# Three mixtures of experts: weighted rows added to the residual in DRAM by indirect DMA, and each tile routed behind its own logits

## The chip, the cores and the metric

The kernel runs on one core of one Trainium2 chip, all in fp32. The metric is the device time of one execution in microseconds (us). The engines are named as the profile names them: PE is TensorE, DVE VectorE, ACT ScalarE, POOL GpSimd; SP is the engine that issues most of the transfers. The core's transfers share 16 DMA engines. SP and ACT issue into hardware queues, POOL into a software queue (q0), which the indirect transfers use.

## The reference

Two transformer blocks on 512 tokens (x, 512x1024) and, in the second block, 256 context tokens. Three times a mixture of 32 experts with top-2 routing stands behind a mixer. Cut to what matters:

```
x = x + hierarchical_moe(rms_norm(x, norm_ffn), ...)          # ma: 512 tokens, no gate
...
f = hier_moe(concat([h2, hc2]), *moe_args)                    # mb: 512 + 256 tokens
x   = x   + g2  * f[:512]
ctx = ctx + cg2 * f[512:]
...
f = hier_moe(h2, *moe_args)                                   # mc: 512 tokens
x = x + g2 * f
return rmsnorm(x, final_g)

def hier_moe(xt, wg, bg, we, be, w1, w3, w2):
    g_idx = argmax(xt @ wg + bg);  g_w = softmax(xt @ wg + bg)[g_idx]     # 4 groups
    top_p, top_e = top_k(softmax((xt @ we + be)[group g_idx]), 2)         # 8 experts each
    weights = g_w * top_p / sum(top_p)
    for each of the two experts e of a token:
        y[token] += weight * ((silu(x @ w1[e]) * (x @ w3[e])) @ w2[e])
```

The gate row g2 (cg2 for the context) has 1024 numbers and is the same for all tokens of its kind.

## The kernel before

The tokens lie in tiles of 128 on the partitions: NT = 4 tiles in ma and mc, 6 in mb (four of x, two of the context). A mixture has a head, a route, a loop over experts and an end.

**Head** (`moe_head`, L269). For each tile, as soon as the mixer before has finished it: norm (`nrm`), transposes (L260), logits on PE (L302), the bias added on DVE into `lg` (L303), and the normed rows stored in DRAM as H (L304); with `keep` the residual rows go to XD in DRAM (L306). The tile scheduler weaves these steps into the mixer's own work.

**Route** (`route`, L498). Once all tiles' logits are in `lg`, one batch of DVE operations on 128 x NT x 32 numbers picks groups and experts, counts with PE matmuls (L570, L574) how many tokens of lower number chose the same expert, and builds with one-hot matrices (L590, L592, matmul L594) tables by expert: `gtab`, which tokens to gather, `tabs`, their weights, `sidx`, where a result row goes, and `cnt`, how many tokens an expert has. The first gather needs `gtab` (cast L625).

**Loop** (`moe`). Per expert 6 MB of weights, six tiles of 1 MB, come by SP's queue into rings of tiles in SBUF (`open_ring`, `pump`): a ring's tile is loaded again when the expert that used it is done. Ahead of the loop the rings fill: 17 tiles in ma, 19 in mb and mc (later some of these tiles are withdrawn for other uses). `gather` fetches the token rows of the expert after next from H by an indirect DMA on POOL (L342), after a clear of the buffer (L348). `block` computes up to 64 tokens: gate and up matmuls (L386), silu (L391, L392), transposes, down matmuls (L404), scaling by the weight on ACT (`yf`, L406), and a scatter of the rows into Y in DRAM by an indirect DMA on POOL (L407). Y has a row for each token and choice, so that no two scatters write the same row. An expert with over 64 tokens runs a second block of 64 or 32 tokens, one with over 128 the loop `later`. In a block of 32 the result is held as 128 partitions x 256.

**End.** Behind expert 29 the loop of mb and mc also reads the residual rows XD into `xr` (L472) and the gate rows `g` into SBUF. After the last scatter each tile reads its two Y rows (L481); DVE adds them (L483) and multiplies by the gate (L484), POOL adds the result to `xr` (L485). In ma the residual has stayed in SBUF and DVE adds both (L487, L488). Then `after` works on each tile: norms for the next stage, or, after mc, the final rmsnorm and the store of the output (L1901, L1902).

The order inside `moe` is that of the code, by a manual schedule; the order outside it, heads and ends among them, is the scheduler's.

Of the kernel before, what the change touches and what calls it, by code (L numbers as in the profile page):

```python
# [6 lines left out]
F32 = mybir.dt.float32  # L7
F32R = mybir.dt.float32r
BF16 = mybir.dt.bfloat16
# [13 lines left out]
class K:  # L23
# [245 lines left out]
    def moe_head(self, tag, NT, wr, br, rows, keep=True, bufs=1):  # L269
# [5 lines left out]
        lg = sp.tile([128, NT, 36], F32, name=tag + "lg")  # L275
# [8 lines left out]
        self.head = tag, NT, st, s2, sp, lg, H  # L284
# [3 lines left out]
        def tile_(t, x, wait=1):  # L288
# [22 lines left out]
    def moe(self, ring, back=None, gate=None, after=None):  # L311
# [5 lines left out]
        tag, NT, st, s2, sp, lg, H = self.head  # L317
        T = NT * 128
        s2.close()
        with st:  # L320
            wk = st.enter_context(tc.tile_pool(reuse_waits="tile", name=tag + "w", bufs=2))
            Y = self.dr.tile([2 * T, D], F32, name=tag + "Y")
            self.ordered = True
            half = lambda n: self.ttile(n, F32)
            self.open_ring(ring, st, 192)
            back_ = (NT + 3) // 4 if gate else 0
            two = lambda n: (self.xtile(n), self.xtile(n))
            self.tleft.clear()
            self.open_ring(6 - (back_ + 1) // 2, self.tpair, 192)
            self.open_ring((back_ + 1) // 2, self.tpair, 192 - 24)  # L330
            if gate:
                self.open_ring(NT // 2, two, 192 - 24)
            if NT == 4:
                self.open_ring(1, two, 192 - 18)

            with ExitStack() as s3:
                rt = s3.enter_context(tc.tile_pool(reuse_waits="tile", name=tag + "r", bufs=1))
                pos, cnt, wid, tabs, sidx, gtab = self.route(tag, rt, sp, lg, NT)
            w2 = st.enter_context(tc.tile_pool(reuse_waits="tile", name=tag + "w2", bufs=1))

# [16 lines left out]
            def block(wk, n, src, xT, wt, si, fill=(), mid=()):  # L357
# [12 lines left out]
                sl = wk.tile([64, 512], F32, name=tag + "sl", tag="sl", bufs=1)  # L370
                sl = [sl[:, 256 * f:256 * f + 256] for f in range(f2)]
                aT = [None] * f2

                def turned(f):
                    pt = self.psumt([128, 128])
                    for k in range(2):
                        nc.tensor.transpose(pt[:, 64 * k:64 * k + 64], sl[f][:, k * 128:(k + 1) * 128], self.ident[0:64, 0:64])
# [32 lines left out]
            def at(i, e):  # L410
                return tabs[:, i, e:e + 1], sidx[:, i, e:e + 1]
# [1545 lines left out]
```

## Time and profile before

| | |
|---|---|
| median of 3 runs | 3354.36 us (3350.82 to 3358.08) |
| profiled execution, own time | 3355.64 us |
| its span in the trace | 3353.8 us |
| mean granted TensorE clock, share of full speed | 0.919 |
| busy: PE, DVE, ACT, POOL | 84%, 33%, 26%, 19% |
| DMA, mean over the span | 250 GB/s |

The profiled execution is 1.84 us longer by its own time than its span in the trace, and 1.3 us above the median of the runs. Busy shares are averages over stages that have different limits: mix1 (to about 670), ma (to 1227), the middle with mix2 (to about 1698), mb (to 2258), mix3 (to about 2722), mc (to 3317) and its end. What a stage waits for is read from windows of it.

### The profile page before, as it was taken

The page shows a single profiled execution, that of the slowest core. Times are in us where ns is not written, and L with a number is a line of the kernel's source. Part 1 is how long each engine was busy: PE and PEld are TensorE (multiplying, and loading weights), DVE is VectorE, ACT ScalarE, POOL GpSimd, SP SyncE. Part 2 cuts the span into 40 slices and gives each one's busy share as a digit, 9 for nine tenths or more (in the row PEclk, how much of TensorE's full clock was granted, in tenths as well). Part 3 has the DMA queues.
Part 4 walks back from the last instruction along what each step waited for, and adds up shares of the span by engine and source line. Part 5 has one row for each costly group of instructions (what it writes and reads, how often), then busy time and mean ns, then how long its engine had stood idle before and what let it go on. Part 6 is the DMA issues. An engine that isn't in the chain of part 4 may idle for free. (4 is left out here: it accounts for less than half of the span.)

```text
span 3353.8 us, 52397 instructions
## 1 busy us (share of the span) xinstructions
PE 2824.7 (84%) x20723; PEld 1945.2 (58%) x20723; DVE 1099.5 (33%) x2328; ACT 860.2 (26%) x1790; POOL 634.1 (19%) x701
## 2 busy tenths in 40 slices
PE   6998898878988879879868998875999867899884
PEld 5766777654544439857744555444877654555442
DVE  3666654331100026555431110116355441010003
ACT  3354211211111126334311111113244311111111
POOL 2111202111211103101012121114122121122111
PEclk7999999969999989969979999996999878999997
DMA  5243358489999973132079999984222273999996
GB/s 185 77 159 121 98 189 273 162 329 411 411 397 398 403 297 117 33 109 70 26 288 406 404 410 384 401 343 141 86 79 60 68 314 152 362 410 391 400 399 241
DMA packets 281904, 838.98 MB, mean 250 GB/s; under 512 B 60002, under 2 KB 118109, under 8 KB 238496
## 3 DMA queue, kind: packets, MB, share of 16 engines
q1 hardware_dynamic: 215872, 752.94, 58.4%
q0 software_dynamic: 32752, 60.57, 4.9%
q10 hardware_dynamic: 32752, 18.80, 2.1%
q8 instruction: 286, 4.69, 0.6%
q14 instruction: 242, 1.98, 0.2%
HBM read 823.93 MB, written 56.59 MB: 263 GB/s over the span
## 5 line engine op out<-in xcount | busy, mean ns | idle before, releaser
L386 PE MATMUL mm<-w,maxT 128*64 128x256 f32 x2048 | 266.4, 396 | 63.7 <-DMA w<-in_w_up_dram 34.6
L386 PE MATMUL mm<-w,mcxT 128*64 128x256 f32 x2048 | 262.8, 399 | 56.0 <-DMA w<-in_moe_w_dram 23.7
L386 PE MATMUL mm<-w,mbxT 128*64 128x256 f32 x2048 | 248.7, 397 | 41.1 <-PEq L455 34.2
L386 PEld LDWEIGHTS mm<-w,maxT 128*64 128x64 f32 x2048 | 157.9, 142 | 174.4 <-DMA w<-in_w_up_dram 51.6
L386 PEld LDWEIGHTS mm<-w,mcxT 128*64 128x64 f32 x2048 | 157.7, 143 | 162.6 <-issue 55.6
L386 PEld LDWEIGHTS mm<-w,mbxT 128*64 128x64 f32 x2048 | 157.4, 142 | 133.1 <-issue 60.5
L246 PE MATMUL mm<-lo,hT 128*128 128x256 f32 x560 | 160.3, 287 | 4.5 <-DVE lo L737 4.4
L244 PE MATMUL mm<-hi,hT 128*128 128x256 f32 x560 | 160.8, 288 | 2.9 <-DVE d_q L149 1.9
L245 PE MATMUL mm<-hi,hT 128*128 128x256 f32 x560 | 160.5, 287 | 0.6 <-DVE hT L202 0.6
L392 DVE TENSOR_TENSOR masl<-masl,mm 64x256 f32<-64x256 f32 x64 | 27.1, 423 | 320.4 <-ACT masl L391 320.4
L392 DVE TENSOR_TENSOR mcsl<-mcsl,mm 64x256 f32<-64x256 f32 x64 | 27.1, 423 | 309.8 <-ACT mcsl L391 309.8
L392 DVE TENSOR_TENSOR mbsl<-mbsl,mm 64x256 f32<-64x256 f32 x64 | 27.0, 423 | 283.9 <-ACT mbsl L391 283.9
L404 PE MATMUL mm<-w,mcaT 128*64 128x512 f32 x512 | 117.1, 599 | 2.7 <-DMA w<-in_moe_w_dram 2.7
L404 PE MATMUL mm<-w,mbaT 128*64 128x512 f32 x512 | 117.1, 599 | 1.7 <-DMA w<-in_moe_w_dram 1.7
L404 PE MATMUL mm<-w,maaT 128*64 128x512 f32 x512 | 117.1, 599 | 0.3 <-DMA w<-in_w_down_dram 0.3
L407 POOL DMA_INDIRECT mbY<-mbyf,mbsidx x38 | 38.0, 1000 | 399.8 <-ACTq L455 148.2
L407 POOL DMA_INDIRECT mcY<-mcyf,mcsidx x35 | 35.1, 1003 | 408.8 <-POOLq L455 163.1
L246 PEld LDWEIGHTS mm<-lo,hT 128*128 128x128 f32 x560 | 107.8, 193 | 5.7 <-DVE lo L737 5.7
L244 PEld LDWEIGHTS mm<-hi,hT 128*128 128x128 f32 x560 | 108.0, 193 | 3.8 <-DVE d_q L149 2.1
L245 PEld LDWEIGHTS mm<-hi,hT 128*128 128x128 f32 x560 | 108.0, 193 | 1.1 <-DVE hT L202 1.0
L245 PE MATMUL mm<-hT,lo 128*128 128x512 f32 x240 | 98.2, 409 | 6.7 <-DVE lo L737 6.6
L407 POOL DMA_INDIRECT maY<-mayf,masidx x32 | 32.7, 1022 | 373.4 <-ACTq L455 195.5
(710 smaller groups left out, 5915.1 us busy)
## 6 DMA issues: line engine op xcount, KB each, us to landing
w<-in_moe_w_dram SPq DMA_DIRECT2D x342, 1024.0 KB
w<-in_w_up_dram SPq DMA_DIRECT2D x64, 1024.0 KB
w<-in_w_down_dram SPq DMA_DIRECT2D x64, 1024.0 KB
w<-in_w_gate_dram SPq DMA_DIRECT2D x57, 1024.0 KB
w<-in_moe_w_dram SPq DMA_DIRECT2D x84, 512.0 KB
w<-in_ada_w_dram SPq DMA_DIRECT2D x34, 1024.0 KB
w<-in_w_in_dram SPq DMA_DIRECT2D x21, 1024.0 KB
w<-in_ada_w_dram SPq DMA_DIRECT2D x28, 512.0 KB
```

What stands on the lines that cost most here:

```text
L244: nc.tensor.matmul(out, l[0], r[0], start=first, stop=False)
L245: nc.tensor.matmul(out, l[1], r[0], start=False, stop=False)
L246: nc.tensor.matmul(out, l[0], r[1], start=False, stop=last)
L386: nc.tensor.matmul(gu[f][n * j:n * j + n], x_[:, k, :], w(j // (q // 2), k)[:, c:c + 256], start=(k == 0), stop=(k == 7))
L392: nc.vector.tensor_tensor(sl[f], sl[f], gu[f][64:128], op=OP.mult)
L404: nc.tensor.matmul(y[n * j:n * j + n], l, w(2, k)[:, c * j:c * j + c], start=(k == 0), stop=(k == 3))
L407: nc.gpsimd.indirect_dma_start(out=Y.rearrange("t (j f) -> (t j) f", f=c), out_offset=bass.IndirectOffsetOnAxis(ap=si, axis=0), in_=yf, in ...
```

## The change

Three things are changed together.

1. **Scatter.** Instead of writing to Y the scatter adds to XD, the residual rows in DRAM (`compute_op=OP.add`), each row as two halves of 512 numbers. So the residual rows are stored in ma too, the weights and the gate row are multiplied in before the scatter (in mc one DVE operation, in mb three, in ma the scaling on ACT as before), with the gate tiles `G` (128x512) loaded by ACT's queue ahead of the loop. Each scatter waits for the one before it, as it did on Y. At the end each tile only reads `xr` from XD, after the last scatter; the reads behind expert 29 are gone.
2. **Route.** `route` becomes a generator for one tile, run right behind the tile's logits in the head. It adds the tile's one-hot products into `acc`; `tables`, ahead of the loop, only turns `acc` into the tables. The two matmuls that count (`pc`) add to the counts of the tiles already routed.
3. **Tiles.** A block of 32 tokens holds its result as 128 partitions x 512 with a clear of `yf` on POOL before; the silu buffer is 128x256; the rings ahead of the loop hold 19 tiles in all three mixtures.

```diff
-            nc.vector.tensor_tensor(lg[:, t, :], pl, bt, op=OP.add)
             nc.gpsimd.dma_start(H[t * 128:(t + 1) * 128, :], h)
-            if keep:
-                self.store(t, x)
-            yield
+            self.store(t, x)
+            yield from self.route(t, pl, bt, rt)
...
-            self.open_ring(6 - (back_ + 1) // 2, self.tpair, 192)
-            self.open_ring((back_ + 1) // 2, self.tpair, 192 - 24)
-            if gate:
-                self.open_ring(NT // 2, two, 192 - 24)
-            if NT == 4:
-                self.open_ring(1, two, 192 - 18)
+            early = 0 if after is None else 1
+            self.open_ring(6 - early, self.tpair, 192)
+            self.open_ring(early, self.tpair, 192 - 24)
+            self.open_ring(2, two, 192)
+            self.open_ring(1, two, 192 - 18)
...
+            for v, row in enumerate(gate or ()):
+                G.append(w2.tile([128, 512], F32, name=f"{tag}G{v}"))
+                for j in range(2):
+                    nc.scalar.dma_start(G[v][64 * j:64 * j + 64], row[512 * j:512 * j + 512].partition_broadcast(64))
...
-                c = 1024 // q
-                y = self.psum([128, c])
+                y = self.psum([128, 512])
...
-                    for j in range(q):
-                        nc.tensor.matmul(y[n * j:n * j + n], l, w(2, k)[:, c * j:c * j + c], start=(k == 0), stop=(k == 3))
-                yf = wk.tile([128, c], F32, name=tag + f"yf{q}", tag="yf")
-                nc.scalar.activation(yf, y, AF.Copy, scale=wt)
-                nc.gpsimd.indirect_dma_start(out=Y.rearrange("t (j f) -> (t j) f", f=c), out_offset=bass.IndirectOffsetOnAxis(ap=si, axis=0),
-                                             in_=yf, in_offset=None, bounds_check=2 * T * q - 1, oob_is_err=False)
+                    for j in range(2):
+                        nc.tensor.matmul(y[64 * j:64 * j + n], l, w(2, k)[:, 512 * j:512 * j + 512], start=(k == 0), stop=(k == 3))
+                yf = wk.tile([128, 512], F32, name=tag + "yf", tag="yf")
+                if n < 64:
+                    nc.gpsimd.memset(yf, 0.0)
+                for r_ in [slice(0, 128)] if n == 64 else [slice(64 * j, 64 * j + n) for j in range(2)]:
+                    if not G:
+                        nc.scalar.activation(yf[r_], y[r_], AF.Copy, scale=wt[0][r_])
+                        continue
+                    nc.vector.scalar_tensor_tensor(yf[r_], y[r_], wt[0][r_], G[0][r_], OP.mult, OP.mult)
+                    if W == 2:
+                        nc.vector.scalar_tensor_tensor(y[r_], y[r_], wt[1][r_], G[1][r_], OP.mult, OP.mult)
+                        nc.vector.tensor_tensor(yf[r_], yf[r_], y[r_], op=OP.add)
+                nc.gpsimd.indirect_dma_start(out=self.XD[0:T].rearrange("t (j f) -> (t j) f", f=512), out_offset=bass.IndirectOffsetOnAxis(ap=si, axis=0),
+                                             in_=yf, in_offset=None, bounds_check=2 * T - 1, oob_is_err=False, compute_op=OP.add)
...
-                if e == 29 and gate:
-                    g = [gate(i, half(f"g{i}")) for i in range(1 + (NT > 4))]
-                    xs = [self.xtile("xr") for _ in range(NT)]
-                    for t in range(NT):
-                        nc.sync.dma_start(xs[t], self.XD[t * 128:(t + 1) * 128, :])
...
             for t in range(NT):
-                a, b = half("y0"), half("y1")
-                for k, o in enumerate((a, b)):
-                    nc.sync.dma_start(o, Y[k * T + t * 128:k * T + t * 128 + 128, :])
-                if gate:
-                    nc.vector.tensor_tensor(a, a, b, op=OP.add)
-                    nc.vector.tensor_tensor(a, a, g[t // 4], op=OP.mult)
-                    nc.gpsimd.tensor_tensor(xs[t], xs[t], a, op=OP.add)
-                else:
-                    nc.vector.tensor_tensor(a, a, b, op=OP.add)
-                    nc.vector.tensor_tensor(xs[t], xs[t], a, op=OP.add)
+                xs.append(self.xtile("xr"))
+                nc.sync.dma_start(xs[t], self.XD[t * 128:(t + 1) * 128, :])
                 ends.append(after(t, xs[t]))
```

The new route, cut to its steps (39 DVE operations a tile; `yield` marks where the scheduler may turn to other work):

```python
    def route(self, t, pl, bt, rt):
...
        nc.vector.tensor_tensor(lg, pl, bt, op=OP.add)
        nc.vector.tensor_reduce(mx, gl, AX.X, OP.max)
        nc.vector.tensor_scalar(ex, gl, mx, None, OP.subtract)
        nc.scalar.activation(ex, ex, AF.Exp, accum_out=gs)
...
        yield
        for k in range(2):
            nc.vector.tensor_reduce(v[:, k:k + 1], m, AX.X, OP.max)
            nc.vector.scalar_tensor_tensor(oh[k], m, v[:, k:k + 1], rev, OP.is_equal, OP.mult)
            nc.vector.tensor_reduce(q[:, k:k + 1], oh[k], AX.X, OP.max)
            nc.vector.tensor_scalar(oh[k], rev, q[:, k:k + 1], None, OP.is_equal)
...
        nc.vector.tensor_tensor(av[:, 2 * i], oh[0], oh[1], op=OP.add)
        pc = self.psum([128, 32])
        nc.tensor.matmul(pc, self.striu, av[:, 2 * i], start=True, stop=(i == 0))
        if i:
            nc.tensor.matmul(pc, self.ones, av[:, 2 * i - 1], start=False, stop=True)
...
        yield
        pw = self.psum([128, 32 * (1 + W)])
        for k in range(2):
            nc.vector.tensor_tensor(big, oh[k], pc, op=OP.mult)
            nc.vector.tensor_reduce(rk[:, k:k + 1], big, AX.X, OP.add)
            nc.vector.tensor_scalar(ohr, self.iota, rk[:, k:k + 1], None, OP.is_equal)
...
            nc.tensor.matmul(pw, ohr, rhs.rearrange("p a b -> p (a b)"), start=(k == 0), stop=(k == 1))
...
            nc.vector.tensor_tensor(accf, accf, pw, op=OP.add)
```

Where instructions stand is shown at three places. The first is PE ahead of mc, where the output projection of mix3 (L244 to L246) for the last tile meets the head's transposes (L260) and logits (L302). Before, the order is:

```order
L302 MATMUL mm<-mcwr,mchT 128x36 [waits DVE_49]
L302 MATMUL mm<-mcwr,mchT 128x36 x3
L244 MATMUL mm<-hi,o_oT_34246 128x512
L245 MATMUL mm<-hi,o_oT_34246 128x512
L246 MATMUL mm<-lo,o_oT_34246 128x512
```

In the change, after the same logits:

```order
L260 MATMUL tr<-c_ident,nh 128x128 [waits DVE_49]
L260 MATMUL tr<-c_ident,nh 128x128 x7
L549 LDWEIGHTS cc_striu
L549 MATMUL mm<-mcav,cc_striu 128x32 [waits DVE_49]
L260 MATMUL tr<-c_ident,nh 128x128 [waits DVE_49,PE_49]
L260 MATMUL tr<-c_ident,nh 128x128 x3
L260 MATMUL tr<-c_ident,nh 128x128 [waits PE_49]
L260 MATMUL tr<-c_ident,nh 128x128
L574 MATMUL mm<-mchT 128x64 [waits DVE_49] x2
L244 MATMUL mm<-hi,o_oT_34287 128x512
L245 MATMUL mm<-hi,o_oT_34287 128x512
L246 MATMUL mm<-lo,o_oT_34287 128x512
```

The routing matmuls of an earlier tile (L549 is `pc`, L574 `pw`), each of which waits for DVE, now stand ahead of output matmuls; before, all routing matmuls stood behind the last logits.

The second place is DVE ahead of ma. Before, between the logits' bias additions (L303) and the table there is one batched route, which begins behind the last tile's addition:

```order
L149 COPY mahT<-tr 128x512 [waits PE_49]
L303 TENSOR_TENSOR malg<-mm,mabr 128x36 [waits PE_49]
L505 TENSOR_REDUCE magm<-malg 128x4 [waits DVE_49]
L509 TENSOR_TENSOR mage<-malg,magm 128x16 [waits DVE_49]
L517 TENSOR_TENSOR mac_6109<-malg,magm 128x16
```

In the change (L519 is the bias addition, the scratch carries the name of the transposes' buffer, mahT) the end of a tile's route, the next tile's logits and a later tile's norm (nrs, nh) follow one another:

```order
L581 TENSOR_TENSOR mapos<-mahT 128x2
L572 TENSOR_TENSOR mahT<-mahT,mawid 128x64 [waits DVE_49] x2
L166 TENSOR_SCALAR nrs<-nss 128x1 [waits Activation_49]
L579 COPY maacc<-mm 128x64 [waits PE_49]
L519 TENSOR_TENSOR mahT<-mm,mabr 128x36 [waits PE_49]
L149 COPY mahT<-tr 128x512 [waits PE_49]
L522 TENSOR_REDUCE mahT<-mahT 128x1 [waits DVE_49]
L169 RECIPROCAL nrs<-nrs 128x1 [waits Activation_49]
L523 TENSOR_SCALAR mahT<-mahT 128x4 [waits DVE_49]
L526 SCALAR_TENSOR_TENSOR mahT<-mahT,c_rev_5882 128x4
L182 SCALAR_TENSOR_TENSOR nh<-x,nrs,rG 128x1024 [waits DMASW0_49,DVE_49]
```

The four routes now run one behind another on DVE, with the norm of the tile after next between them.

The third place is DVE behind mb's loop, where the norms of mix3 (rs, nf) begin. Before:

```order
L483 TENSOR_TENSOR y_34157<-y_34157 128x1024 [waits DMAHW6_49,DMAHW4_49,DMAHW0_49]
L238 TENSOR_TENSOR lo<-w,hi 128x2048 [waits DMAHW6_49,DMAHW2_49,Activation_49]
L484 TENSOR_TENSOR y_34157<-y_34157,g_33439 128x1024 [waits DVE_49]
L483 TENSOR_TENSOR y_34166<-y_34166 128x1024 [waits DMAHW5_49,DMAHW6_49,DMAHW4_49,DMAHW2_49]
L238 TENSOR_TENSOR lo<-w,hi 128x2048 [waits DMAHW6_49,DMAHW2_49,Activation_49]
L484 TENSOR_TENSOR y_34166<-y_34166,g_33439 128x1024 [waits DVE_49]
L166 TENSOR_SCALAR rs<-nss 128x1 [waits Activation_49]
```

In the change:

```order
L166 TENSOR_SCALAR rs<-nss 128x1 [waits Activation_49]
L238 TENSOR_TENSOR lo<-w,hi 128x2048 [waits DMAHW4_49,DMAHW2_49,DMAHW6_49,DMAHW0_49,Activation_49]
L166 TENSOR_SCALAR rs<-nss 128x1 [waits Activation_49]
L169 RECIPROCAL rs<-rs 128x1 [waits Activation_49]
L166 TENSOR_SCALAR rs<-nss 128x1 [waits Activation_49]
L169 RECIPROCAL rs<-rs 128x1 [waits Activation_49]
```

The additions and the gate's products are gone; the norms of all six tiles (rs) stand directly behind the loop, ahead of the first nf operation (L197).

## Rows read from the trace of the kernel before

**Rows 1.** The page: busy us and instructions, then DMA share and GB/s in 40 slices

```profile
PE 2824.7 (84%) x20723; PEld 1945.2 (58%) x20723; DVE 1099.5 (33%) x2328; ACT 860.2 (26%) x1790; POOL 634.1 (19%) x701
...
DMA  5243358489999973132079999984222273999996
GB/s 185 77 159 121 98 189 273 162 329 411 411 397 398 403 297 117 33 109 70 26 288 406 404 410 384 401 343 141 86 79 60 68 314 152 362 410 391 400 399 241
```

**Rows 2.** Windows by stage: columns in the first line

```profile
core 0: us, PE busy (x) PEld busy (x) DVE busy (x) ACT busy (x) POOL busy (x), PEclk, DMA share, GB/s
...
720.00:740.00 20.00, 19.22 (x131) 11.14 (x131) 2.70 (x5) 4.32 (x8) 1.84 (x2) 0.89 0.26 92
740.00:1225.00 485.00, 417.60 (x2808) 226.03 (x2804) 46.48 (x92) 74.71 (x184) 88.39 (x90) 0.98 1.00 399
...
1760.00:2258.00 498.00, 440.59 (x3266) 246.52 (x3260) 50.28 (x114) 82.43 (x204) 91.25 (x92) 0.97 0.99 395
2258.00:2330.00 72.00, 26.11 (x137) 22.16 (x138) 47.87 (x69) 28.18 (x49) 36.59 (x30) 0.62 0.37 131
...
2750.00:2880.00 130.00, 100.23 (x740) 58.67 (x740) 13.27 (x36) 17.09 (x41) 14.99 (x15) 0.85 0.55 215
2880.00:3317.00 437.00, 379.60 (x2580) 206.80 (x2572) 42.35 (x83) 68.56 (x168) 80.09 (x81) 0.97 0.98 389
```

**Rows 3.** The timeline behind mc's last scatter: start, duration, engine, operation [idle before]

```profile
3316.89 0.98 POOL L407 DMA_INDIRECT mcY<-mcyf,mcsidx  x1 [16.62 <-POOLq L455]
3319.42 0.82 SPq L481 DMA_DIRECT2D y<-mcY  x2
...
3324.61 1.23 DVE L483 TENSOR_TENSOR y<-y 128x1024 f32<-128x1024 f32 x1 [12.71 <-DMA y<-mcY]
...
3344.69 1.06 ACT L164 ACTIVATE y<-xr 128x1024 f32<-128x1024 f32 x1 [4.65 <-POOL xr L485]
...
3349.43 0.33 SPq L1902 DMA_DIRECT2D out_dram<-y  x1
```

**Rows 4.** The timeline of POOL behind mb's last scatter

```profile
2257.74 0.98 POOL L407 DMA_INDIRECT mbY<-mbyf,mbsidx  x1 [17.50 <-ACTq L455]
2271.69 3.24 POOL L485 TENSOR_TENSOR xr<-xr,y 128x1024 f32<-128x1024 f32 x1 [12.96 <-DMA y<-mbY]
...
2297.24 2.36 POOL L485 TENSOR_TENSOR xr<-xr,y 128x1024 f32<-128x1024 f32 x1 [1.50 <-DVE rs L166]
```

**Rows 5.** Groups of DVE from 2262 to 2325: busy us, mean ns | idle before

```profile
L484 DVE TENSOR_TENSOR y<-y,g 128x1024 f32<-128x1024 f32 x6 | 11.0, 1837 | 0.1
...
L483 DVE TENSOR_TENSOR y<-y 128x1024 f32<-128x1024 f32 x6 | 7.9, 1308 | 4.3 <-DMA y<-mbY 4.3
```

**Rows 6.** DMA: a queue's packets, MB, share; then issues, their count, size

```profile
q0 software_dynamic: 32752, 60.57, 4.9%
...
xr<-XD SPq DMA_DIRECT2D x10, 512.0 KB
...
g<-mods SPq DMA_DIRECT2D x3, 512.0 KB
```

**Rows 7.** The timeline of POOL in ma's loop, a scatter and the clear behind it

```profile
749.84 1.02 POOL L407 DMA_INDIRECT maY<-mayf,masidx  x1 [8.39 <-POOLq L455]
752.31 0.95 POOL L348 MEMSET maxg<- 128x1024 f32 x1 [1.46 <-DMA maY<-mayf,masidx]
```

**Rows 8.** The timeline of DVE in ma's route, beginning and table

```profile
697.07 0.17 DVE L505 TENSOR_REDUCE magm<-malg 128x4 f32<-128x16 f32 x1
697.28 0.17 DVE L509 TENSOR_TENSOR mage<-malg,magm 128x16 f32<-128x16 f32 x1
...
710.41 0.19 DVE L623 TENSOR_SCALAR matk<-mm 128x32 f32<-128x32 f32 x1 [0.83 <-PE mm L594]
...
710.86 0.18 DVE L625 CAST magtab<-matk 128x32 int32<-128x32 f32 x1
```

**Rows 9.** The line of the logits' addition: duration ns, first and last start

```profile
L303 DVE TENSOR_TENSOR malg<-mm,mabr x4: 195/196/196, 678.7 to 696.8; 128x36 f32<-128x36 f32 x4
L303 DVE TENSOR_TENSOR mclg<-mm,mcbr x4: 196/196/198, 2700.0 to 2722.1; 128x36 f32<-128x36 f32 x4
```

More of the change, by code (lines that the diff above doesn't have):

```diff
@@ L369, in block @@
                 gu = [self.psum([128, 256]) for _ in range(f2)]
-                sl = wk.tile([64, 512], F32, name=tag + "sl", tag="sl", bufs=1)
-                sl = [sl[:, 256 * f:256 * f + 256] for f in range(f2)]
+                sl = wk.tile([128, 256], F32, name=tag + "sl", tag="sl", bufs=1)
+                sl = [sl[64 * f:64 * f + 64] for f in range(f2)]
                 aT = [None] * f2
@@ L560, in route @@
+        nc.vector.tensor_tensor(wid[:, t, 1, a:a + 1], den, e1, op=OP.mult)
         for k in range(2):
-            for t in range(NT):
-                for i in range(2):
-                    nc.vector.tensor_scalar(wid[:, t, k, 1 + i:2 + i], self.part, float(t * 128 + 1 + i * k * T), None, OP.add)
-        av = r([128, NT, 32], "av", BF16)
-        nc.vector.tensor_tensor(av, oh[0], oh[1], op=OP.add)
-        pc = self.psum([128, NT * 32])
-        for t in range(NT):
-            for u in range(t + 1):
-                nc.tensor.matmul(pc[:, t * 32:(t + 1) * 32], self.striu if u == t else self.ones, av[:, u, :], start=(u == 0), stop=(u == t))
@@ L572, in route, with tables @@
+        accf = acc.rearrange("p a b -> p (a b)")
+        if i:
+            nc.vector.tensor_tensor(accf, accf, pw, op=OP.add)
+        else:
+            nc.vector.tensor_copy(accf, pw)
+        nc.vector.tensor_scalar(q, q, -EB, 32.0 * EB, OP.mult, OP.add)
+        nc.vector.tensor_tensor(pos[:, t, :], q, rk, op=OP.add)
+        yield
+    def tables(self, tag, rp, sp, rt):
+        nc = self.nc
+        pos, wid, acc, av, done = rt
+        W = acc.shape[1] - 1
         pcn = self.psum([1, 32])
-        for t in range(NT):
-            nc.tensor.matmul(pcn, self.ones[:, 0:1], av[:, t, :], start=(t == 0), stop=(t == NT - 1))
+        nc.tensor.matmul(pcn, self.ones[:, 0:1], av[:, 2 * len(done) - 1], start=True, stop=True)
@@ L586, in route @@
-        pw = self.psum([128, 96])
-        for k in range(2):
-            for t in range(NT):
-                ohr = rp.tile([128, 128], F32, name=tag + "ohr", bufs=2)
-                nc.vector.tensor_scalar(ohr, self.iota, rk[:, t, k:k + 1], None, OP.is_equal)
-                rhs = rp.tile([128, 3, 32], F32, name=tag + "rhs", bufs=2)
-                nc.vector.tensor_tensor(rhs, oh[k][:, t, :].unsqueeze(1).to_broadcast([128, 3, 32]),
-                                        wid[:, t, k, :].unsqueeze(2).to_broadcast([128, 3, 32]), op=OP.mult)
-                nc.tensor.matmul(pw, ohr, rhs.rearrange("p a b -> p (a b)"), start=(k == 0 and t == 0), stop=(k == 1 and t == NT - 1))
@@ L1891, in result, with back @@
         G, rs = [], k.cm.tile([128, 8], F32, name="rs", tag="rs")
-        def gains(i, t):
-            G.append(k.ttile("fG", F32))
-            nc.sync.dma_start(G[0], A["final_g_2"].partition_broadcast(128))
-            return gain_rows(1)(i, t)
+        def back(last):
+            if not last:
+                G.append(k.ttile("fG", F32))
+                nc.sync.dma_start(G[0], A["final_g_2"].partition_broadcast(128))
         def after(t, x):
@@ L1902, in after @@
             nc.sync.dma_start(A["out"][0, t * 128:(t + 1) * 128, :], o)
-        return gains, after
-    def gain_rows(l):
-        def gains(i, t):
-            nc.sync.dma_start(t, k.mods[i, l, 5120:6144].partition_broadcast(128))
-            return t
-        return gains
+        return back, after
     for l in range(2):
-        moe(RING[1 + l], None, *(result() if l and stop is None else (gain_rows(l),)))
+        back, after = result() if l and stop is None else (None, None)
+        moe(RING[1 + l], back, [k.mods[i, l, 5120:6144] for i in range(2 - l)], after)
         if stop == f"moe{l + 2}":
```

186 lines of the change are left out of this document (82 added, 104 removed).

## The prediction

> **What bounds the kernel now.** I read the page's busy shares and its 40 slices first. TensorE is busy 84% of the span, but the DMA line shows three long plateaus at 9 with about 400 GB/s [rows 1]: the expert loops of the three mixtures. The windows by stage say which limit holds in each. In ma's loop (740 to 1225) the 16 DMA engines are busy 1.00 of the time, in mb's (1760 to 2258) 0.99, in mc's from 2880 on 0.98, while TensorE works 418 of 485, 441 of 498 and 380 of 437 us [rows 2]: these loops go at the speed of the weights, and each further megabyte in them costs about 2.5 us. The other three windows are of another kind. At ma's start (720 to 740) the DMA engines work 0.26 of the time: the rings of weight tiles are full, and nothing moves until the first expert has used a tile. From 2750 to 2880 mc is short of neither: TensorE 100 of 130, DMA 0.55, a chain of early large experts in which each step waits for the one before. Behind mb's last expert (2258 to 2330) TensorE works 26 of 72 us and VectorE 48 [rows 2]. So there are three places to win or lose: bytes in the loops, the route ahead of a loop (what is lost while the rings stand full), and the tails behind them.
>
> **The change, part by part.** The sum is made against the profiled execution, 3355.6 us; the median of the runs is 3354.4, 1.3 below it, which I carry over at the end.
>
> *Tails.* In mc's tail the last scatter starts at 3316.89, the reload of the result rows is issued 2.5 us later at 3319.42, the first addition on VectorE starts at 3324.61, 5.2 behind the issue; the last tile's square starts at 3344.69, its store is issued at 3349.43, and 4.4 us later the span ends [rows 3]. Between 3324.6 and 3344.7 stand, per tile, two operations on VectorE and one on POOL, all gone in the change: a tile then needs one reload. Four reloads of 0.52 MB at some 400 GB/s take 5.2 us, the last row is there at about 3319.4 + 2.5 + 5.2 = 3327; from square to store it needs the old 4.7 us, then 4.4: 3336. With 1.5 us for a slower landing of the accumulating scatter 3337.5, **-16.5**. In mb's tail the last scatter starts at 2257.74, POOL's first residual addition at 2271.69, its sixth at 2297.24 for 2.36 us [rows 4]; the twelve VectorE operations between them (L483, L484) take 7.9 + 11.0 = 18.9 us [rows 5] on the engine that is the busiest of this window [rows 2]. With them gone the norms of all six tiles stand ahead of the first nf operation, and what is left on VectorE (47.9 - 18.9 = 29 us) starts when the first row is there, at about 2265. I take **-19** (bounds: -12, if the weight splits and transposes that share the tail set its end; -29, the time by which the last x is earlier, 2299.6 against 2271). In ma the four tiles' two operations are gone too, but TensorE has the next stage's projection to do in the meantime: **-3** (0 to -5).
>
> *Loops.* Before, the residual rows (xr) and the gate rows (g), 0.52 MB each, are read inside the loop, behind expert 29: six and two in mb, four and one in mc [rows 6]. The reload now stands behind the last scatter, and of the gates half-wide tiles (0.26 MB each) are loaded at the loop's start. That frees (8 - 1) x 0.52 = 3.7 MB in mb and (5 - 0.5) x 0.52 = 2.4 MB in mc; at 395 and 389 GB/s [rows 2] **-9.3** and **-6.0**.
>
> *The accumulating scatter.* Rows scattered: 2 x (512 + 768 + 512) = 3584 of 4 KB, 14.7 MB. The software queue's packets, scatters among them, take 4.9% of 16 engines' span, 164 us for 60.57 MB [rows 6]; the scatters' part by bytes is 40 us. No row shows an accumulation. Below: nothing more than now, 0, since bytes out of SBUF are the same. Above, from the same row: an element that reads its target and writes it is a gather and a scatter, +40. A plain element has two legs, read and write; one that adds has three. Half of 40 is nearest to that, and nearly all of it falls in loops that have no idle DMA: **+20**. The Trainium skill (DMA: Bandwidth & Descriptors, Rules for kernel authors) states that an accumulating DMA reads its destination and writes it later with nothing that holds the bytes in between, so that the next one has to wait for its semaphore. No row here shows such a read; by that sentence the third leg is real and the sum is the one with +20, without it the sum would be 20 lower. The wait is no new one: already now the scatter of a plain row is followed by a clear on POOL that started 1.46 us late because of it [rows 7], and the gather behind it is two experts ahead. A few us more of landing hide there.
>
> *The route.* A tile's route is 39 VectorE operations, some 25 of which depend on the one before. Dependent small ones start 0.21 apart (697.07, 697.28), and a wait for a routing matmul costs up to 0.83 [rows 8]: 25 x 0.21 + 8 x 0.12 + 3 x 0.4 = about 7.5 us. In ma the logits come from 678.7 to 696.8 [rows 9], the table of tokens is done at 711.04 [rows 8]. VectorE now does four routes one behind another from the first logits on, with two norms, three copies and small ones between (5.5) and 1.1 of tables: 678.7 + 30 + 5.5 + 1.1 = 715.3, **+4.3**. Against this the rings ahead of ma's loop hold 19 tiles instead of 17, 2.1 MB that come in the time that stands idle now, at 399 GB/s **-5.3**; ma's rows must now be stored (2.1 MB) but that too falls into the 15 idle us of 720 to 740 [rows 2]. In mb six tiles are routed; five are done before the last logits, so behind these one route and the tables stay, 8.6 instead of more than 14 (711.0 - 696.8); with six tiles' wider operations I take 18 for the old one, so 10 gained, and 5 given back by TensorE, whose order now has pc and pw, which wait for VectorE, ahead of the last tile's output matmuls: **-5**. In mc the logits come 7.4 apart (2700.0 to 2722.1 [rows 9]), no slower than VectorE routes, and I allow three such waits of 3 us on the chain to the last tile: 5.5 gained, 9 lost, **+3.5**. mc's early experts are a chain: wider result rows with a clear on POOL for blocks of 32, and a longer landing, **+3** (0 to +8).
>
> *Sum.* ma 4.3 - 5.3 - 3 = -4; mb -5 - 9.3 - 19 = -33.3; mc 3.5 + 3 - 6.0 - 16.5 = -16; together -53.3, with +20 for the accumulation -33.3: 3322.3, or 3321 against the median.
>
> **Rivals.**
> (a) *The accumulation is dear.* If an element that adds holds its DMA engine until the target's row is back, it is not the bytes that count. It decides from +53 us on, that is where a scatter takes 2.3 times the engine time of a plain one. At three times it is +80: 3382, slower. For it: the loops have no slack at all (DMA 0.98 to 1.00). Against it: a scatter's 128 rows are 8 for each of 16 engines, so that one row's read can lie beside another's write, and the weights' transfers come between.
> (b) *Routing becomes the bound of the stages ahead.* Ten tiles in mb and mc, each with three waits of TensorE in its own order; 2 us lost per tile is +20: 3341. The logits' spacing in mc (7.4, as long as a route) speaks for it; that TensorE has other tiles' matmuls to do speaks against it.
> (c) *The tails are covered.* mb's tail then waits for the next stage's weights and their splits, mc's for the scatters' landing: half of 38.5 remains, 3340; together with an accumulation at the upper bound 3360, no change.
> The edits surely take effect: the operations of the tails are gone from the order.
>
> **How the numbers follow.** My forecast 0.50, (a) 0.17, (b) 0.17, (c) 0.16. Within the first the range is 3302 (accumulation at 0) to 3343 (at +40). To hold 8 in 10 I reach down to 3298 (tails at their lower bounds with some accumulation) and up past (b) and (c) to 3362, which leaves out most of (a) and little below. What a measurement can tell from no change is about 0.2%, 6.7 us. Faster: all of the forecast, of (b) and (c) four fifths: 0.76; the same: 0.08, from (c) and the mild part of (a); slower: 0.16, the rest of (a).
>
> **What would show it.** In the tails: mc's span from last scatter to end near 20 us instead of 36.9, mb's gap on TensorE some 19 us shorter, with no POOL additions. In the loops: the software queue's share up from 4.9% by 0.6 if +20 holds, by more than 1.6 points if (a) does, and the loops' lengths with it. Ahead of the loops: the first gather of ma 4 us later, of mb earlier. I am wrong if the loops grow by over 40 us, or if the gather of mc is over 10 us later.

## The result: 1.2% slower, and the profile after

The changed kernel takes 3394.8 us (median; 3392.45 to 3420.5) against 3353.8 us of the kernel before on the same chip: a ratio of 1.012, with a 95% interval of 1.0089 to 1.0152. I had forecast 3321, and the range ended at 3362. The profiled execution has a span of 3391.9 us, 38.1 more than before.

The page's busy shares hardly move. The DMA queues do: the software queue's share is 6.5%, where it was 4.9% [rows 6].

```profile
PE 2843.7 (84%) x20616; PEld 1959.3 (58%) x20616; DVE 1194.7 (35%) x2723; ACT 831.8 (25%) x1744; POOL 671.9 (20%) x700
...
q0 software_dynamic: 40272, 62.69, 6.5%
```

Where the time went is best read from landmarks: the first and last logits matmul (L302) of a mixture, the cast of its gather table, its first and last scatter, the end. The next rows are of the changed kernel, each a line of the view by tile: the shortest, median and longest duration in ns, then first and last start in us.

```profile
L302 PE MATMUL mm<-mawr,mahT x64: 268/407/426, 676.8 to 720.0; 128*128 128x36 f32 x64
L302 PE MATMUL mm<-mbwr,mbhT x96: 198/407/430, 1538.0 to 1752.3; 128*128 128x36 f32 x96
L302 PE MATMUL mm<-mcwr,mchT x64: 193/337/408, 2735.8 to 2779.9; 128*128 128x36 f32 x64
L616 DVE CAST magtab<-matk x1: 181/181/181, 728.9 to 728.9; 128x32 int32<-128x32 f32 x1
L616 DVE CAST mbgtab<-mbtk x1: 182/182/182, 1761.1 to 1761.1; 128x32 int32<-128x32 f32 x1
L616 DVE CAST mcgtab<-mctk x1: 182/182/182, 2788.8 to 2788.8; 128x32 int32<-128x32 f32 x1
L415 POOL DMA_INDIRECT XD<-mayf,masidx x32: 1573/1590/1638, 755.1 to 1255.2; - x32
L415 POOL DMA_INDIRECT XD<-mbyf,mbsidx x38: 1542/1569/1612, 1790.2 to 2316.8; - x38
L415 POOL DMA_INDIRECT XD<-mcyf,mcsidx x35: 1542/1569/1607, 2816.7 to 3370.4; - x35
```

The same landmarks of the kernel before, which rows 9 give only in part (DVE's addition behind the logits):

```profile
L302 PE MATMUL mm<-mawr,mahT x64: 267/407/426, 674.7 to 696.4; 128*128 128x36 f32 x64
L302 PE MATMUL mm<-mbwr,mbhT x96: 198/407/429, 1505.0 to 1697.2; 128*128 128x36 f32 x96
L302 PE MATMUL mm<-mcwr,mchT x64: 193/279/429, 2696.6 to 2721.6; 128*128 128x36 f32 x64
...
L407 POOL DMA_INDIRECT maY<-mayf,masidx x32: 1008/1024/1042, 736.4 to 1227.5; - x32
L407 POOL DMA_INDIRECT mbY<-mbyf,mbsidx x38: 985/1001/1029, 1743.2 to 2257.7; - x38
L407 POOL DMA_INDIRECT mcY<-mcyf,mcsidx x35: 978/1004/1029, 2763.6 to 3316.9; - x35
```

Subtracting neighbours (the tables of before were cast at 710.9, 1716.0 and 2736.1) gives a balance that adds up to the 38.1 us:

| stretch | before | after | difference |
|---|---|---|---|
| start to ma's first logits | 674.7 | 676.8 | +2.1 |
| first to last logits: ma, mb, mc | 21.7, 192.2, 25.0 | 43.2, 214.3, 44.1 | +21.5, +22.1, +19.1 |
| last logits to gather table: ma, mb, mc | 14.5, 18.8, 14.5 | 8.9, 8.8, 8.9 | -5.6, -10.0, -5.6 |
| table to first scatter: ma, mb, mc | 25.5, 27.2, 27.5 | 26.2, 29.1, 27.9 | +0.7, +1.9, +0.4 |
| first to last scatter: ma, mb, mc | 491.1, 514.5, 553.3 | 500.1, 526.6, 553.7 | +9.0, +12.1, +0.4 |
| ma's last scatter to mb's first logits | 277.5 | 282.8 | +5.3 |
| mb's last scatter to mc's first logits | 438.9 | 419.0 | -19.9 |
| mc's last scatter to the end | 36.9 | 21.5 | -15.4 |

So the ends of mb and mc are shorter, as forecast. The route behind the last logits is shorter too. But first and last logits lie 19 to 22 us further apart, and the loops of ma and mb, relieved of reads, are longer.

Why the logits are late stands in TensorE's waits, here ahead of ma (672 to 738). Columns: us in total, times, longest.

```profile
PE mm L549 <- DVE maav L547: 19.5, 4, 7.8
PE tr L260 <- DMA maxg<-maH,magtab: 10.1, 1, 10.1
PE tr L260 <- DVE nh L182: 5.0, 2, 3.2
PE tr L260 <- DVE mahT L527: 2.5, 1, 2.5
PE mm L574 <- DVE mahT L571: 2.5, 3, 0.8
```

L549 is `pc`, the count of a tile. Before, such a wait stood there once, behind all logits (6.9 us); now four of them take 19.5, and behind all but the last (4.8 us) other tiles' work is queued. TensorE's timeline shows what:

```profile
680.54 1.52 PE L260 MATMUL tr<-c_ident,nh 128*128 128x128 f32 x6
689.86 0.21 PE L549 MATMUL mm<-maav,cc_striu 128*128 128x32 bf16 x1 [7.79 <-DVE maav L547]
691.85 1.52 PE L260 MATMUL tr<-c_ident,nh 128*128 128x128 f32 x6 [1.78 <-DVE nh L182]
693.16 0.95 PE L574 MATMUL mm<-mahT 128*128 128x64 f32 x4
693.91 3.57 PE L302 MATMUL mm<-mawr,mahT 128*128 128x36 f32 x16
...
714.85 0.19 PE L549 MATMUL mm<-maav,cc_striu 128*128 128x32 bf16 x1 [4.22 <-DVE maav L547]
```

Between two tiles' logits TensorE stands for a count that VectorE has not finished, and then VectorE stands for the logits (1.4 to 3.4 us a tile, 11.1 in all; before it was 11.5, but without routes in between): the two take turns. VectorE's order has its part in it: of the longest wait, 7.8 us, VectorE itself stood 3.7 for ScalarE, for the norm of a later tile that lies in the middle of the first tile's route. Ahead of mb and mc the waits for counts are smaller (6.8 and 11.9 us); there TensorE also waits longer than before for norms that stand in VectorE's order among route steps (mb: 19.0 us from 1533 to 1758, 13.7 from 1500 to 1703 before), and in the same windows it is busy 10.8 us longer, as the routing matmuls now lie among the logits.

The end of mc, where the stretch of rows 3 held eight reloads, the additions and the products, is now this (start, duration, engine, operation):

```profile
3370.37 1.54 POOL L415 DMA_INDIRECT XD<-mcyf,mcsidx  x1 [13.82 <-POOLq L463]
3374.15 1.77 SPq L483 DMA_DIRECT2D xr<-XD  x4
3377.83 1.06 ACT L164 ACTIVATE out<-xr 128x1024 f32<-128x1024 f32 x1 [11.94 <-DMA xr<-XD]
...
3386.66 1.28 DVE L1893 SCALAR_TENSOR_TENSOR out<-xr,rs,fG 128x1024 f32<-128x1024 f32 x1
```

The reload is issued 3.8 us behind the scatter's start, where it was 2.5: it waits for the scatter, so the accumulation lands some 1.3 us later, 0.6 of it by the longer issue on POOL (1.54 against 0.98). In the loops of ma and mb the DMA engines are as busy as in rows 2, and move less:

```profile
760.00:1253.00 493.00, 422.27 (x2798) 232.79 (x2796) 46.33 (x91) 76.63 (x184) 105.63 (x89) 0.94 1.00 388
...
1810.00:2315.00 505.00, 444.85 (x3186) 244.72 (x3185) 129.66 (x212) 59.51 (x166) 113.13 (x94) 0.97 0.99 379
```

388 and 379 GB/s at shares of 1.00 and 0.99, where it was 399 and 395.

### The profile page after: what moved, and what is told of

The parts are those of the page before. It is cut to its first block, busy times and chain, and to the rows that moved or that the text cites. A ratio compares the mean times of both kernels' runs of the same rounds, so it can differ in the third digit from the quotient of the medians.

```text
span 3391.9 us, 52474 instructions
## 1 busy us (share of the span) xinstructions
PE 2843.7 (84%) x20616; PEld 1959.3 (58%) x20616; DVE 1194.7 (35%) x2723; ACT 831.8 (25%) x1744; POOL 671.9 (20%) x700
## 3 DMA queue, kind: packets, MB, share of 16 engines
q0 software_dynamic: 40272, 62.69, 6.5%
## 5 line engine op out<-in xcount | busy, mean ns | idle before, releaser
L386 PEld LDWEIGHTS mm<-w,maxT 128*64 128x64 f32 x2048 | 165.0, 147 | 173.5 <-issue 60.9
L246 PE MATMUL mm<-lo,hT 128*128 128x256 f32 x560 | 160.7, 288 | 5.1 <-DVE lo L728 4.9
L244 PE MATMUL mm<-hi,hT 128*128 128x256 f32 x560 | 161.2, 289 | 3.0 <-DVE d_q L149 1.9
L415 POOL DMA_INDIRECT XD<-mbyf,mbsidx x38 | 59.6, 1568 | 415.5 <-DVEq L463 144.2
L415 POOL DMA_INDIRECT XD<-mcyf,mcsidx x35 | 54.9, 1568 | 409.4 <-DVEq L463 174.2
L415 POOL DMA_INDIRECT XD<-mayf,masidx x32 | 51.0, 1594 | 371.8 <-ACTq L463 200.0
L246 PEld LDWEIGHTS mm<-lo,hT 128*128 128x128 f32 x560 | 108.4, 194 | 6.5 <-DVE lo L728 6.5
L244 PEld LDWEIGHTS mm<-hi,hT 128*128 128x128 f32 x560 | 108.3, 194 | 3.9 <-DVE d_q L149 2.1
L244 PE MATMUL mm<-hT,hi 128*128 128x512 f32 x240 | 99.7, 416 | 1.7 <-ACT hi L727 1.1
```

The costliest lines, as they stand in the source:

```text
L244: nc.tensor.matmul(out, l[0], r[0], start=first, stop=False)
L246: nc.tensor.matmul(out, l[0], r[1], start=False, stop=last)
L386: nc.tensor.matmul(gu[f][n * j:n * j + n], x_[:, k, :], w(j // (q // 2), k)[:, c:c + 256], start=(k == 0), stop=(k == 7))
L415: nc.gpsimd.indirect_dma_start(out=self.XD[0:T].rearrange("t (j f) -> (t j) f", f=512), out_offset=bass.IndirectOffsetOnAxis(ap=si, axis=0 ...
```

## The experiments

My first theory after the result: the route costs some 45 us by TensorE's waits, the accumulation some 40 in the loops, and the ends give 35 back. Rivals: all of the loss is in the loops; or the accumulation is free and something else in the loops is slow. Ratios are against the kernel before on the same chip; as the runs come from several chips, gains between two kernels are read from their ratios, and stretches from their traces.

**Plain scatters everywhere.**

```diff
-                                             in_=yf, in_offset=None, bounds_check=2 * T - 1, oob_is_err=False, compute_op=OP.add)
+                                             in_=yf, in_offset=None, bounds_check=2 * T - 1, oob_is_err=False)
```

> The change with plain scatters: each expert's weighted row overwrites the residual row instead of being added to it (so the sums are left out; bytes, waits and instructions are the same). Theory: against the kernel before, the first scatter comes 18.7 us later in ma, and the three loops lost 9.6, 14.0 and 0.8 us although two of them were relieved of 15 us of reads and the first of 5 by deeper rings; so an accumulation costs some 40 us over a plain write. Then this run takes about 3355, the software queue's share falls back from 6.5% to about 5.0%. First rival: the price is the 20 us that I forecast, and the rest of the loops' loss is something else: 3375. Second rival: the accumulation costs nothing, the loops lose by the wider result rows: 3395.

Measured: 3391.2 us, 1.0092 (1.0056 to 1.0127). By the total the accumulation would be nearly free. But the total doesn't price it, as its scatters show:

```profile
L415 POOL DMA_INDIRECT XD<-mbyf,mbsidx x39: 969/996/1018, 1779.0 to 2317.9; - x39
L415 POOL DMA_INDIRECT XD<-mcyf,mcsidx x36: 971/998/1018, 2816.8 to 3370.2; - x36
L415 POOL DMA_INDIRECT XD<-mayf,masidx x32: 1011/1019/1033, 757.0 to 1244.6; - x32
```

With the sums left out the later mixtures route other rows: 39 and 36 scatters instead of 38 and 35, so that mb and mc are other work. Only ma's loop can be compared, with 32 scatters in both: 487.6 us against 500.1, so 12.5 us for the accumulation there. A run that changes the data behind which a branch is chosen is no clean price; the next two mend that.

**Plain scatters in mc alone.**

```diff
-                                             in_=yf, in_offset=None, bounds_check=2 * T - 1, oob_is_err=False, compute_op=OP.add)
+                                             in_=yf, in_offset=None, bounds_check=2 * T - 1, oob_is_err=False, **({} if tag == "mc" else {"compute_op": OP.add}))
```

> The change with plain scatters in mc alone (mc's sums are left out; nothing behind mc is routed, so that all blocks are those of the change, which the run with plain scatters everywhere was not: one block more in mb and in mc). Theory: an accumulating scatter takes more time of the DMA engines than a plain one, 12.5 us in ma's loop (500.1 against 487.6 us from first to last scatter), and about as much in mc: 3395 - 13 = 3382. Rival: the accumulation is nearly free, since plain scatters everywhere took 3391: no change, 3392 to 3395.

Measured: 3386.4 us, 1.0077 (1.006 to 1.0095), by the ratios some 14 us below the change, though the intervals overlap. The loop decides: mc's takes 544.1 instead of 553.7, where four other kernels with the accumulation, rows of 2 KB and a per-tile route took 553.2 to 553.5. The 9.6 us are the accumulation's price in this mc. The rival (free) falls. So does the other one, that the loops lose by the wider result rows: with plain scatters the loops of ma and mc are no longer than before (487.6 and 544.1 us against 491.1 and 553.3).

**The accumulation alone, on the kernel before.**

```diff
+    z = k.cp.tile([128, 128], F32, name="zero")
+    nc.vector.memset(z, 0.0)
...
+            nc.scalar.dma_start(k.Y[tag][t * 128:t * 128 + 128, :].rearrange("p (a f) -> p a f", f=128), z.unsqueeze(1).to_broadcast([128, 8, 128]))
...
-                                             in_=yf, in_offset=None, bounds_check=2 * T * q - 1, oob_is_err=False)
+                                             in_=yf, in_offset=None, bounds_check=2 * T * q - 1, oob_is_err=False, compute_op=OP.add)
```

> The kernel before with one thing changed: the scatters add to Y, which is set to zero during mix1 (14.7 MB of writes while the DMA engines are half idle). Every row is still written once, and ends, route and rings are those of before. Theory: the accumulation costs some 3% of the DMA-bound loops' bandwidth, about 40 us in all three: 3355 + 40 = 3395, and the software queue's share goes up by 1.5 points. Rival: it is nearly free, 3357.

Measured: 3455.4 us, 1.0281 (1.0264 to 1.0298), 60 more than expected. Most of that is the setting to zero, which I had taken for hidden: it stands ahead of the first weights (in the first 100 us TensorE works 15.8 us where it worked 65.9), and ma's first logits come at 731.8 instead of 674.7. The price is in the loops, and those can be read:

```profile
L407 POOL DMA_INDIRECT maY<-mayf,masidx x32: 1565/1593/1641, 794.4 to 1297.1; - x32
L407 POOL DMA_INDIRECT mbY<-mbyf,mbsidx x38: 1552/1579/1621, 1818.4 to 2346.8; - x38
L407 POOL DMA_INDIRECT mcY<-mcyf,mcsidx x35: 1546/1579/1622, 2853.2 to 3412.0; - x35
```

502.7, 528.4 and 558.8 us against 491.1, 514.5 and 553.3: +11.6, +13.9, +5.5, together **31 us** (in mc less than the 9.6 of the run above). The queue's own time:

```profile
q0 software_dynamic: 39696, 60.59, 6.2%
```

6.2% of 3449.9 is 214 us for the bytes that took 164: about 50 us more, part of it where the DMA engines have time to spare (mc's early experts). Its packets go from 32752 to 39696 at the same counted bytes.

**Rows of 4 KB instead of 2 KB** (on the deferred route below; ma and mc alone).

```diff
+                if W == 1:
+                    yf = wk.tile([64, 1024], F32, name=tag + "yf", tag="yf", bufs=1)
...
+                    nc.gpsimd.indirect_dma_start(out=self.XD[0:T], out_offset=bass.IndirectOffsetOnAxis(ap=si[0:n], axis=0),
+                                                 in_=yf[0:n], in_offset=None, bounds_check=T - 1, oob_is_err=False, compute_op=OP.add)
```

> The deferred route with rows of 4 KB in the scatters of ma and mc (64 rows x 1024 numbers where it was 128 x 512; mb as it is). Theory A: the price of the accumulation goes by rows (descriptors), so it is halved in ma and mc, some 12 us less: 3362 - 12 = 3350. Theory B: it goes by bytes: 3362, or a few us more for two evictions of a block.

Measured: 3367.1 us, 1.0026 (1.001 to 1.0042), against 1.0003 with 2 KB. The loops take 497.6 and 558.6 where they took 499.8 and 553.2, so ma's is 2.2 us shorter and mc's 5.4 longer. The software queue has 35856 packets instead of 40272, and its share is 6.4% in the place of 6.5%. Fewer and longer rows make it no cheaper: theory A falls. That the price goes by bytes, theory B, agrees with this; mc's 5.4 us stay unexplained.

**The batched route back, accumulation kept.** The route of the kernel before, with its result in the new tables.

```diff
-            yield from self.route(t, pl, bt, rt)
+            nc.vector.tensor_tensor(rt[:, t, :], pl, bt, op=OP.add)
+            yield
```

> The change with the route of the kernel before: the logits of all tiles are collected, and one batch of operations routes them ahead of the loop; the accumulating scatter, the shorter ends and the rings stay. Theory: the per-tile route costs 18 us ahead of ma, and some 15 ahead of mb and 13 ahead of mc (gather tables 18.0 later in ma; 17.4 later in mb counted from ma's last scatter; in mc 6.4 earlier, where the end of mb alone should give 19), because TensorE's order holds routing matmuls that wait for VectorE ahead of other tiles' logits: about 3350. Rival: the route is hidden as forecast, and the loss is all in the loops: 3390 to 3395.

Measured: 3367.6 us, 1.0022 (1.0004 to 1.0041): about 33 us below the change (1.2% less 0.2%). First to last logits take 23.4, 192.6 and 25.1 us again, as before, and with the stretch from last logits to table 39.8 us are given back. Part of it is lost again behind the tables: mc's loop takes 561.7 us where it took 553.7, mb's 531.1 where it took 526.6, and the profiled execution is only 25.4 us shorter. The route's price ahead of the loops is real, somewhat smaller than the 45 expected.

**The per-tile route alone, on the kernel before.**

```diff
-            nc.vector.tensor_tensor(lg[:, t, :], pl, bt, op=OP.add)
...
-            yield
+            yield from self.route(t, pl, bt, lg)
```

> The kernel before with the per-tile route alone: plain scatters into Y and the old ends stay. Theory: the route's price of about 45 us adds to the kernel before: 3400. The rival that the route is hidden says 3354; if the price comes only together with the stores of the residual rows in ma, it is about 3382.

Measured: 3395.6 us, 1.0098 (1.0066 to 1.013), some 33 us. The total is no clean price: in the profiled execution 19.7 us of the loss lie ahead of ma's first logits (see the end). The stretches are clean. First to last logits take 42.0, 213.5 and 44.3, and with the stretch to the table that is 40.0 us more than before: the route stretches the logits with or without the accumulation. The loops take 490.4, 511.9 and 548.9: those of ma and mb move little, mc's is 4.4 us shorter.

**The route held back by one tile.**

```diff
-            yield from self.route(t, pl, bt, rt)
+            lag.append(self.route(t, pl, bt, rt))
+            next(lag[-1])
+            yield
+            while len(lag) > (len(GS2) < NT):
+                yield from lag.pop(0)
```

> The change with each tile's route held back until the next tile's logits are in TensorE's order. Theory: a part of the waits of TensorE goes, a third of 45 us: about 3380. If the price is not TensorE's waits but VectorE's work and the activation table's loads, it stays at 3395.

Measured: 3361.6 us, 1.0003 (0.9985 to 1.0022). The same work on VectorE (2723 instructions, 1192.5 us busy against 1194.7), by the ratios some 39 us less: over twice the 15 that I expected. The logits of the kernel with the deferred route, and TensorE's waits for the counts ahead of ma:

```profile
L303 PE MATMUL mm<-mawr,mahT x64: 268/408/429, 678.6 to 711.7; 128*128 128x36 f32 x64
L303 PE MATMUL mm<-mbwr,mbhT x96: 198/407/429, 1532.2 to 1729.7; 128*128 128x36 f32 x96
L303 PE MATMUL mm<-mcwr,mchT x64: 196/279/407, 2717.1 to 2748.1; 128*128 128x36 f32 x64
```

```profile
PE mm L555 <- DVE maav L553: 8.8, 4, 2.9
```

33.1, 197.5 and 31.0 us from first to last, where the change has 43.2, 214.3 and 44.1; the last logits to the tables take 5.4 us more, so 34.6 of the 41.5 us are gone. The four waits for counts are 8.8 us instead of 19.5. So the price is the place of the route in the engines' order, not the amount of VectorE's work. The edit moves the route's steps on VectorE as well as the counts on TensorE; which of the two weighs more it does not tell apart.

**Which mixture gains.** The deferred route with the batch in ma:

```diff
+            if tag == "ma":
+                nc.vector.tensor_tensor(rt[:, t, :], pl, bt, op=OP.add)
+                yield
+                return
             lag.append(self.route(t, pl, bt, rt))
```

> The deferred route in mb and mc, and in ma the batched one: gather tables of ma came at 714.0 with the batch and at 723.0 with the deferred route, so some 9 us less than the deferred route alone: 3362 - 9 = 3353. Rival: what is saved ahead of ma's loop is lost in its first experts, because the rings have had less time to fill: 3362.

Measured: 3350.3 us, 0.9973 (0.9957 to 0.9988), as the theory says. Then ma wholly as before (the old functions under other names), and ma and mb wholly as before:

```diff
-            k.moe(*a)
+            (k.moe_b if k.head[0] in OLD else k.moe)(*a)
```

> ma entirely as in the kernel before (batched route, plain scatters into Y, rows held in SBUF); mb and mc with the accumulating scatter and the deferred route. Theory: in ma the accumulation has only a price (11.6 us in the loop, and an end that is no shorter: 485.6 us from ma's last scatter to mb's tables against 488.5), so against the run with ma routed as a batch some 12 us are gained: 3350 - 12 = 3338. Rival: what ma's loop wins is lost again, since its rings hold two tiles less and the rows wait in SBUF: 3350.

Measured, with OLD = ma: **3336.0 us, 0.993 (0.9911 to 0.995)**, as expected; the rival (3350) falls.

> ma and mb entirely as in the kernel before; mc alone with the accumulating scatter and the deferred route. Theory by the stages of the runs so far: mc gains 15 us at its end and 6 in its loop, and pays 6 to 10 for the accumulation; its deferred route costs nothing against the batch (462.3 against 463.9 us): 3357 - 13 = 3344. In mb gain (15 at the end, 9 in the loop) and price (14 for the accumulation, 8 that I can't explain) cancel, so the two kernels of this pair lie within some 6 us of each other. Rival: mb's share is a gain of 15 or more; then this kernel is that much slower than its neighbour.

Measured, with OLD = ma and mb: 3354.1 us, 0.9983 (0.9963 to 1.0002). The rival is right: mb brings some 18 us (0.993 against 0.9983), not nothing. The interval reaches 1, so a gain of mc alone is not shown. And the same as the best with the batched route:

> The kernel with ma as before and the accumulating scatter in mb and mc, now with the batched route in all three. Theory A: held back by one tile, the per-tile route is a gain in mb and mc: between the run with batched routes and the one with the deferred route in mb and mc lie 7 us ahead of mb's tables, 5 in mb's loop, 3 ahead of mc's and 8 in mc's loop; so 3336 + 20 = 3356. Theory B: the deferred route only costs less than the one behind the logits, and those differences are the scatter between executions: 3336, or 8 us less, since mc's tables came 8 us later in the kernel with mc alone changed (486.7 against 478.4 us from mb's last scatter).

Measured: 3343.1 us, 0.9949 (0.9927 to 0.997). The 20 us of theory A are not there. Whether the deferred route is better at all these runs do not settle: the intervals overlap, but the medians, taken on the same chip, lie 7 us apart in its favour, and mc's loop takes 558.7 us with the batch against 553.5. What the run does show is that the accumulating scatter in mb and mc, with the shorter ends that it allows, is a gain of 0.5% without any change of the route.

## Why the prediction was wrong, step by step

- **The route: the step that failed.** I let the logits stand where they were and put the routes beside them: "VectorE now does four routes one behind another from the first logits on", and "no slower than VectorE routes" for mc. What lies behind the last logits came as worked out: -5.6, -10.0 and -5.6 where I had taken -10 for mb and -5.5 for mc. What I had not let follow is that the counts wait in TensorE's own order ahead of the next tiles' transposes and logits. I allowed 5 us for it in mb, 9 in mc and nothing in ma; the stretch of the logits grew by 22.1, 19.1 and 21.5. A route by itself has the length that I gave it: the last tile's in ma runs on VectorE from 720.41 to 727.87, 7.5 us. The route costs +41.5 us in the balance, not +2.8. That its place in the order is the cause is shown by the deferred route, and that it needs no accumulation by the route alone. Rival (b) named the mechanism, at half its size and a chance of 0.17.
- **The accumulation: right in kind, too small.** I took 20 us, with 40 as the upper end. The loops pay 31, the engines 50. The guess by legs (read, read, write) was too low: by the queue's time the added rows cost 40 + 50 us where the plain ones cost 40 (my estimate by bytes), some 2.2 times, near the 2.3 of rival (a). Its mechanism, a price that does not go by bytes, has no support in the run with rows of 4 KB. In time the price is smaller in each loop, and smallest in mc (5.5 or 9.6 us), whose early experts leave the DMA engines time to spare; that this is why is argued. The Trainium skill (DMA: Bandwidth & Descriptors, Rules for kernel authors) states that an accumulating DMA reads its destination; the queue's time, 214 us for 164, agrees with it.
- **The relief of the loops: too large.** Deeper rings in ma, and reads moved out in mb and mc, should have given 20.6 us, less 3 for wider rows in mc. With 31 for the accumulation the loops (with the stretch from table to first scatter) should have grown by 13; they grew by 24.5. In ma half of the 5.3 is there (500.1 against 502.7 with the accumulation alone; with the per-tile route and plain scatters 487.6 against 490.4). In mb a fifth of the 9.3 (526.6 against 528.4), which the spread hides: seven other kernels with this loop took 525.7 to 531.1. In mc the 5.1 us between 558.8 (accumulation alone) and 553.7 are no proof of the 6.0, because the route differs too: with the batched route in both nothing is left (558.8 alone, 561.7 and 558.7 with the reads moved out), with the per-tile route and plain scatters 4.8 (548.9 and 544.1). That the route itself shortens mc's loop (553.3 to 548.9 with the route alone) I had not foreseen, and no run tells why. Where mb's other 7 us went stays open as well.
- **The ends.** mc: -15.4 for -16.5. mb: -19.9 for -19. Both right, with the steps named. ma: +5.3 for -3. There the rows had stayed in SBUF, and now they must come back from DRAM behind the last scatter; I had priced the additions that go and not the reload that comes. The runs bear the reload out in kind and not in size: seven kernels that reload these rows take 277.6 to 282.8 us for that stretch, six that keep them in SBUF 274.1 to 277.8, on average 4 us less.
- **The sum.** -33.3 forecast, +38.1 in the profile: 71.4 off, of which the route 38.7, the loops 22.1, ma's end 8.3, the rest 2.3.

The chance of 0.16 for slower rested on rival (a) alone. The accumulation stayed within the bounds that I gave it. The route did not: its 38.7 us alone turn -33.3 into +5.4, and the loops and ma's end make that a clear loss. The signs I had named show it: ma's table came 18.0 us later and not 4, mb's later and not earlier (17.4 us counted from ma's last scatter), and mc's 52.7 later, where I had set 10 as the sign of being wrong. The software queue's share rose by 1.6 points, the edge I had set for rival (a), though part of that is ma's residual rows, which POOL now stores (2.1 MB).

## What to carry to other kernels

Work that is split by tile and moved to the side of an in-order engine is paid where that engine waits for it: look at what stands behind each new wait in the order, and let those instructions move before a sum is made; holding the work back by one tile can take most of the price away. An accumulating DMA into DRAM saves reloads and additions at a loop's end, and pays for it, in rows of 4 KB as of 2 KB, for as long as the loop is DMA-bound: here it was worth it in mb and mc together, whose ends became 19.9 and 15.4 us shorter, and a loss in ma, where the rows were in SBUF anyway (0.9973 with ma changed, 0.993 without). The best kernel of this study keeps ma as it was and takes the accumulation with a deferred route in mb and mc: 0.993; with the batched route it is 0.9949, which the intervals do not tell apart.

## What the runs showed that I had not expected

An accumulating scatter of 14.7 MB in 106 DMAs took about 50 us more of the 16 engines than the plain one; longer rows (4 KB for 2 KB in ma and mc) did not make it cheaper. Its issue on POOL took 1.57 us instead of 1.00. It landed only some 1.3 us later (3.8 against 2.5 us from scatter to reload).

The stage ahead of all changed instructions moves by itself. In the run with the route alone ma's first logits came at 694.4 instead of 674.7, with the same code in mix1; in the other kernels that leave mix1 as it is they came at 673.4 to 684.3. The loss lies between 460 and 540. Ahead of it, from 380 to 460, TensorE worked 73.7 of 80 us in that run and 74.0 in the kernel before, at a granted clock of 0.98 in both. Then the clock fell, to a mean of 0.66 between its two levels (0.5 is 1.2 GHz, 1 is 2.4 GHz), where the kernel before had 0.89, and in the same time TensorE did 1295 matmuls instead of 1621. The rows are the window 460 to 540 of that run and of the kernel before, with the columns of rows 2:

```profile
460.00:540.00 80.00, 76.73 (x1295) 60.08 (x1295) 21.01 (x33) 8.71 (x19) 11.60 (x20) 0.66 0.64 212
```

```profile
460.00:540.00 80.00, 76.98 (x1621) 63.72 (x1623) 31.41 (x53) 12.00 (x24) 19.39 (x31) 0.89 0.81 272
```

Why it fell in that execution stays open. So a single span says little within 20 us; the stretches between landmarks behind it do.
